# A two-layer attention encoder on one core: layer B's bias rows built by GpSimd, its bias loads in four transfers, and several steps of layer B moved

## The chip, the cores and the metric

The kernel runs on one core of a Trainium2 chip. The core has a matrix engine (PE), VectorE (DVE), ScalarE (ACT), GpSimd (POOL) and a queue engine (SP, SyncE), each with its own stream of instructions worked off in order, and 16 DMA engines. The metric is the device time of one execution in microseconds; lower is better.

## The reference

One sequence of 512 tokens of width 1024 goes through two layers. Each normalises its input, projects it to queries, keys, values and a gate, mixes by attention with 16 heads of 64, multiplies by silu(gate), projects back and adds the residual. Layer A attends in three dilated windows; layer B, the one that the change is mostly about, attends in a window of 8 by 16 on an 8 by 64 grid:

```python
def mixer_b(hn, w_in, w_out, q_gain, k_gain, rpb):
    proj = hn @ w_in
    q, k, v, gate = jnp.split(proj, 4, axis=-1)
    q = rms_norm(q..., q_gain) * (HEAD_DIM ** -0.5)
    k = rms_norm(k..., k_gain)
    ...
    bias = col_bias[:, row_idx].transpose(0, 2, 3, 1, 4)      # from rpb, by relative row and column
    logits = jnp.einsum('bhcqd,bhrcjd->bhcqrj', qr, kr).astype(jnp.float32) + bias
    logits = jnp.where(col_valid[:, :, None, :], logits, NEG_INF)
    p = softmax(logits)
    out = jnp.einsum('bhcqrj,bhrcjd->bhcqd', p, vr)
    ...
    y = y * jax.nn.silu(gate)
    return y @ w_out
```

All is float32.

## The kernel before

Every large product is made of three matmuls: each factor is split into a high part, rounded, and a low part, the rest (`wh`, `wl` of the raw weights `wraw`; `hn_h`, `hn_l` of the normalised input; the two halves of `y`), and the three products that matter are added in PSUM. ACT rounds the high parts of weights (L136), DVE or GpSimd subtracts for the low ones (L142). All matmuls go through one helper, L231.

The 16 heads form eight pairs, called hc 0 to 7. PE's order is written by hand with a clock of the plan: each matmul issued adds its estimated nanoseconds, and the attention of the pairs (the side work) is woven into the projections (the main work). `later_on(delay, job)` issues a job when that clock has advanced by `delay`; `B_PLAN` lists, for layer B, when the `scores` and the `values` of each pair come, in nanoseconds after layer B's start. The other engines' order comes from a scheduler, except where `tc.keep_in_program_order` pins an instruction. Nearly all DMAs are issued from SP's one queue, in order; each also waits for a DMA eight places before it to have landed.

In layer B a pair goes through these steps. Its Q and K are normalised (`head_norm`, on GpSimd or, with `quick`, with the root on DVE), written to DRAM (`bd<-rawq`, L738) and read back transposed (`rawq<-bd` or `vv<-bd` by the tile's name, L744; both in `move_b`). `side_b` scales the keys into `kx` on ACT (L776), copies two end blocks of `kx` (L1247), and after a time of the plan issues the scores (`log<-kx`, 64 small matmuls). DVE adds the bias `eb` and takes the maximum (L1275), ACT takes the exponential and divides (L1285, L1290). P is transposed (`turn_b`), written to `tdb` (L1225) and read back as `pt` (L1230). `values` then are `weigh` (`o<-pt`) and `put_y`: ACT and DVE copy and add the output (L791, L792), DVE multiplies by the gate (L846, tiles `gt` or `gx`), ACT rounds y's high part (L849), GpSimd or DVE subtracts for the low part (L852). y is a factor of the output projection at the end of the layer.

The bias `eb` (two buffers, by hc % 2) is read for one pair by eight DMAs of 80 KB (`eb<-eb_d`, L881, `bias_b`), issued at the start of the pair before. `eb_d`, in DRAM, is put together once during layer A by `bias_rows`: the table is loaded as `rp`, negated, widened by a fill value, written to two DRAM buffers, and 14 DMAs from DRAM to DRAM, one every 12000 ns of the plan, lay out its blocks.

The last residual (`pt<-xm_d`, L1173) is read in two halves into the halves of the `pt` buffer that P^T of pairs 6 and 7 leave. `tr` is the buffer, a single one, in which layer A's transposed P are gathered before they are written.

Of the kernel before, what the change touches and what calls it, by code (L numbers as in the profile page):

```python
# [22 lines left out]
P = 128  # L23
# [3 lines left out]
NHC = 8  # L27
# [19 lines left out]
    ("scores", 0, 47700), ("scores", 1, 70000), ("values", 0, 82000), ("scores", 2, 87000),  # L47
    ("values", 1, 108000), ("scores", 3, 108700), ("values", 2, 117000), ("scores", 4, 125400),
    ("scores", 5, 145000), ("values", 3, 145000), ("scores", 6, 165000), ("values", 4, 166000),
    ("scores", 7, 176700), ("values", 5, 180000), ("values", 6, 198000), ("values", 7, 207000),  # L50
# [5 lines left out]
def tile_hybrid_encoder(  # L56
# [39 lines left out]
    lb_d = dr.tile([P, 376], F32, name="lb_d")  # L96
    gb_d = dr.tile([P, 248], F32, name="gb_d")
    eb_d = dr.tile([P, 4, EB], F32, name="eb_d")
# [362 lines left out]
    def bias_rows():  # L461

        rp = wk.tile([P, 248], F32, tag="eg", name="rp")
        tc.keep_in_program_order(nc.sync.dma_start(rp, rpb))
        nc.gpsimd.tensor_scalar(rp, rp, -1.0, None, op0=ALU.mult)
        lb = wk.tile([P, 376], F32, tag="eg", name="lb")
        nc.gpsimd.memset(lb, BIG)
        nc.gpsimd.tensor_copy(lb[:, 15 * 8 : 31 * 8], rp[:, 7 * 8 : 23 * 8])
        nc.sync.dma_start(gb_d, rp)
        nc.sync.dma_start(lb_d, lb)  # L470

        far, near = (lb_d, 376), (gb_d, 248)
        jobs = [(2 * W5 + W5 * n, W5, far, 120) for n in range(4)]
        jobs += [(o, 32, far, 24) for o in (0, W5, 7 * W5 - 32, 8 * W5 - 32)]
        jobs += [(32, 32, near, 216), (64, 96, near, 120), (W5 + 32, P, near, 88)]
        jobs += [(6 * W5, P, near, 56), (7 * W5, 96, near, 56), (7 * W5 + 96, 32, near, 24)]

        def spread_out(o, n, src, at):
            t, width = src
            dst = bass.AP(eb_d.tensor, eb_d.offset + o, [[4 * EB, P], [EB, 4], [1, n]])  # L480
            src = bass.AP(t.tensor, t.offset + at, [[width, P], [-8, 4], [1, n]])
            tc.keep_in_program_order(nc.sync.dma_start(dst, src))

        for n, job in enumerate(jobs):
            later_on(30000 + 12000 * n, partial(spread_out, *job))
# [23 lines left out]
    def project_qk(n, ns, key, hc, guard, first=False, **kw):  # L509
# [219 lines left out]
    def move_b(hc):  # L729
# [17 lines left out]
        out, back = (6000, 13500) if hc % 2 else (14000, 20500)  # L747
# [73 lines left out]
    def put_y(hc, o, permuted, last):  # L821
# [33 lines left out]
        if permuted and hc < NHC - 3:  # L855
            later_on(9000, finish)
        else:
            finish()
# [14 lines left out]
    def bias_b(hc):  # L873

        def load(j, hd):
            src = bass.AP(
                eb_d.tensor,
                eb_d.offset + (2 * hc + hd) * 32 * EB + (0, 2, 2, 4)[j] * W5,
                [[EB, 4], [4 * EB, 8], [1, 4 * W5]],
            )  # L880
            tc.keep_in_program_order(nc.sync.dma_start(st["eb"][32 * j : 32 * j + 32, hc % 2, hd, :], src))  # L881

        for j in range(4):
            for hd in range(2):
                load(j, hd)
# [35 lines left out]
    def attn_a(hc):  # L921
# [115 lines left out]
        if hc < NHC - 1:  # L1037
            for u in range(2):
# [199 lines left out]
    def side_b(hc):  # L1238
        if hc >= 1 and hc + 1 < NHC:
            bias_b(hc + 1)  # L1240
# [6 lines left out]
        nc.gpsimd.tensor_copy(sb(kx, 0, [[576, 2], [1, 64]]), sb(kx, 128, [[320, 2], [1, 64]]))  # L1247
        yield 3500
# [67 lines left out]
        later_on(7500, partial(send_b, hc, pt))  # L1316
        pending.append(lambda: put_y(hc, weigh(), False, hc == NHC - 1))
# [25 lines left out]
    def side():  # L1343
# [22 lines left out]
        for hc in range(NHC):  # L1366
            if hc < NHC - 1:
# [147 lines left out]
```

## Time and profile before

| | |
|---|---|
| time, median of 3 runs | 810.78 us (814.51, 810.78, 810.58) |
| profiled execution, its own time | 816.14 us |
| its span | 814.3 us |
| mean granted clock of PE | 0.996 |
| PE busy | 799.7 us (98%) |
| DVE, ACT, POOL busy | 527.0, 441.3, 228.8 us |
| DMA | 172.14 MB, mean 211 GB/s |

The span is the profiled execution from its first to its last instruction; 1.84 us of its time lie around it. The profiled execution was 5.36 us longer than the median of the others. Busy time counts work of an engine; waits are listed apart, by what ended them.

### The profile page before, as it was taken

How to read it: one execution, taken by the hardware profiler on the slowest of the kernel's cores; microseconds unless marked ns; L12 is line 12 of the kernel's file. 1: busy time of each engine (PE TensorE's matmuls, PEld its weight loads, DVE VectorE, ACT ScalarE, POOL GpSimd, SP SyncE). 2: the span in 40 equal slices, each digit the busy share in tenths (PEclk: the TensorE clock that was granted, in tenths of full speed). 3: DMA queues.
4: the chain of work that ended last, by engine and by line, in shares of the span. 5: the costliest groups of instructions: out<-in, count | busy, mean ns of one | idle time of the engine just before them, and what ended most of it. 6: DMA issues, size and time to landing. Idle time of an engine off the chain costs nothing. (4 is left out here: it accounts for less than half of the span.)

```text
span 814.3 us, 17799 instructions
## 1 busy us (share of the span) xinstructions
PE 799.7 (98%) x6718; PEld 655.7 (81%) x6718; DVE 527.0 (65%) x1398; ACT 441.3 (54%) x925; POOL 228.8 (28%) x373
## 2 busy tenths in 40 slices
PE   9999999999999999999999999999999998999887
PEld 7888888888888888888888888888888786878776
DVE  7474575675675675676676776557648777786634
ACT  7442745645645745745746575454346666656520
POOL 2242432432442432432433232120403133220100
PEclk9999999999999999999999999999999999999999
DMA  8579578768987987877978963284556696777663
GB/s 288 159 205 259 149 220 257 232 195 234 247 225 215 293 243 217 260 221 220 283 212 238 282 179 113 61 280 155 176 158 168 209 220 199 237 214 216 199 171 145
DMA packets 96694, 172.14 MB, mean 211 GB/s; under 512 B 16288, under 2 KB 52272, under 8 KB 96608
## 3 DMA queue, kind: packets, MB, share of 16 engines
q1 hardware_dynamic: 96464, 170.74, 71.3%
q8 instruction: 53, 0.87, 0.5%
q10 hardware_dynamic: 144, 0.26, 0.1%
q14 instruction: 33, 0.27, 0.1%
HBM read 128.36 MB, written 48.24 MB: 217 GB/s over the span
## 5 line engine op out<-in xcount | busy, mean ns | idle before, releaser
L231 PE MATMUL acc<-wh,hn_h 128*128 128x512 f32 x704 | 278.2, 396 | 0.4 <-ACT hn_h L419 0.4
L231 PE MATMUL acc<-wl,hn_h 128*128 128x512 f32 x704 | 274.3, 390 | 0.2 <-POOL wl L142 0.2
L231 PE MATMUL acc<-wh,hn_l 128*128 128x512 f32 x704 | 274.2, 390 | 0.0
L136 ACT CAST wh<-wraw 128x512 fp32r<-128x512 f32 (+1 forms) x258 | 157.7, 614 | 211.7 <-PE acc L231 184.1
L142 DVE TENSOR_TENSOR wl<-wraw,wh 128x512 fp32r<-128x512 f32 (+2 forms) x187 | 136.9, 733 | 159.6 <-ACT wh L136 159.0
L142 POOL TENSOR_TENSOR wl<-wraw,wh 128x512 fp32r<-128x512 f32 (+1 forms) x72 | 96.5, 1340 | 227.0 <-ACT wh L136 177.6
L231 PEld LDWEIGHTS acc<-wh,hn_h 128*128 128x128 f32 x704 | 132.6, 189 | 32.6 <-issue 4.2
L231 PEld LDWEIGHTS acc<-wh,hn_l 128*128 128x128 f32 x704 | 132.4, 188 | 27.9
L231 PEld LDWEIGHTS acc<-wl,hn_h 128*128 128x128 f32 x704 | 132.7, 188 | 27.4 <-POOL wl L142 0.9
L309 POOL TENSOR_TENSOR sq<-rawq 128x256 f32<-128x256 f32 (+1 forms) x82 | 59.9, 739 | 110.4 <-ACT rawq L540 97.9
L231 PE MATMUL acc<-y,wh 128*128 128x512 f32 (+1 forms) x272 | 82.3, 386 | 2.0 <-ACT y L849 1.8
L992 ACT ACTIVATE p<-p,mn 128x512 f32<-128x512 f32 (+1 forms) x64 | 44.9, 702 | 60.2 <-DVE mn L981 60.2
L231 PE MATMUL acc<-hn_h,wh 128*128 128x512 f32 x192 | 75.8, 395 | 1.5 <-ACT rawk L540 1.5
L231 PE MATMUL acc<-hn_h,wl 128*128 128x512 f32 x192 | 74.8, 390 | 0.0
L231 PE MATMUL acc<-hn_l,wh 128*128 128x512 f32 x192 | 74.8, 389 | 0.0
L310 DVE TENSOR_REDUCE ss<-sq 128x4 f32<-128x256 f32 (+1 forms) x96 | 47.6, 506 | 32.2 <-POOL sq L309 31.7
L231 PEld LDWEIGHTS acc<-y,wh 128*128 128x128 f32 x272 | 49.0, 189 | 12.2 <-ACT y L849 2.2
L231 PE MATMUL acc<-y,wl 128*128 128x512 f32 (+1 forms) x136 | 51.4, 378 | 0.0
L329 DVE TENSOR_TENSOR rawq<-rawq,rs 128x256 f32<-128x256 f32 (+1 forms) x96 | 48.2, 563 | 2.3 <-POOL rs L128 1.9
L540 ACT ACTIVATE rawq<-acc,rs_n 128x512 f32<-128x512 f32 (+1 forms) x76 | 46.1, 613 | 0.5
L900 DVE STREAM_TRANSPOSE tr<-p 128x512 f32<-128x512 f32 x56 | 39.0, 706 | 11.4 <-ACT p L812 11.4
L812 ACT ACTIVATE p<-p,mn 128x512 f32<-128x512 f32 (+1 forms) x64 | 44.4, 701 | 2.1 <-DVE mn L811 2.1
(140 smaller groups left out, 911.4 us busy)
## 6 DMA issues: line engine op xcount, KB each, us to landing
wraw<-in_w SPq DMA_DIRECT2D x121, 512.0 KB
td<-tr SPq DMA_DIRECT2D x14, 1024.0 KB
pt<-td SPq DMA_DIRECT2D x56, 256.0 KB
qd<-rawq SPq DMA_DIRECT2D x7, 1536.0 KB
qt<-qd SPq DMA_DIRECT2D x28, 384.0 KB
tdb<-tb SPq DMA_DIRECT2D x8, 768.0 KB
pt<-tdb SPq DMA_DIRECT2D x32, 192.0 KB
eb<-eb_d SPq DMA_DIRECT2D x64, 80.0 KB
```

The source lines that it names most:

```text
L136: nc.scalar.copy(h, raw)
L142: eng.tensor_sub(l, raw, h.bitcast(F32))
L231: nc.tensor.matmul(o, l, r, **kw)
L309: nc.gpsimd.tensor_mul(to, v, v)
L310: nc.vector.tensor_reduce(ss[:, i * ns : (i + 1) * ns], sq.rearrange("p (a b) -> p a b", b=64), axis=AX.X, op=ALU.add)
L329: m = nc.vector.tensor_mul(v, v, by)
L540: nc.scalar.activation(dst, src, AF.Copy, scale=rs_n[:, i : i + 1])
L812: nc.scalar.activation(pr, pr, AF.Copy, scale=mn[:, 3:4])
L900: nc.vector.transpose(dst, src[:, :n].rearrange(order, b=4, k=32, **({"g": 2} if apart else {})))
L992: nc.scalar.activation(row, row, AF.Exp, bias=mn[:, 1:2], scale=-1.0, accum_out=mn[:, 2:3])
```

## The change

- `bias_rows(cq)` is called four times in layer A, once for each of four blocks of columns, behind the second half of the attention of hc 2 to 5. It loads the table into a tile in the `tr` buffer, and 4000 ns later GpSimd fills the 1280 columns of bias rows beside it: one memset, seven negating copies. 16000 ns after the start one DMA of 640 KB writes them to `eb_d`. The two DRAM buffers and the 14 DMAs are gone.
- `bias_b` reads a pair's bias in four DMAs of 160 KB, and is issued 4000 ns after the pair before last (the one that used the same buffer) is through its softmax.
- In `side_b` the end blocks of `kx` are copied by ACT, pinned in order, and 5000 ns of the plan lie between the keys and the scores, before 3500.
- For pairs 6 and 7 the second `head_norm` comes 11500 ns after its cause, before 18000, with its root on DVE. Pair 7's read back comes 12500 ns on, before 13500.
- `put_y` of layer B rounds y 4000 ns later, for pairs 0 to 5.
- The first half of the last residual is read behind pair 7's read of P^T, before: behind pair 6's values.
- `B_PLAN` has other times.

```diff
@@
 )
 B_OUT = B_IN + 4 * KT * D
 B_PLAN = (
-    ("scores", 5, 145000), ("values", 3, 145000), ("scores", 6, 165000), ("values", 4, 166000),
-    ("scores", 7, 176700), ("values", 5, 180000), ("values", 6, 198000), ("values", 7, 207000),
...
+    ("scores", 5, 143500), ("values", 3, 151500), ("scores", 6, 160500), ("values", 4, 168000),
+    ("scores", 7, 171500), ("values", 5, 182000), ("values", 6, 193000), ("values", 7, 199000),
 )
 W_COLS = B_OUT + KT * D
 
@@
     l0_d = dr.tile([16, P, 256], F32, name="l0_d")
     lines_d = dr.tile([16, 2, 448], F32, name="lines_d")
     l12_d = dr.tile([16, 2, 32, 224], F32, name="l12_d")
-    lb_d = dr.tile([P, 376], F32, name="lb_d")
-    gb_d = dr.tile([P, 248], F32, name="gb_d")
-    eb_d = dr.tile([P, 4, EB], F32, name="eb_d")
+    eb_d = dr.tile([16, 32, EB], F32, name="eb_d")
 
     v0x = cp.tile([P, 1024], F32, name="v0x")
     v0 = [v0x[:, 512 * i : 512 * i + 512].rearrange("p (i c) -> p i c", i=4) for i in range(2)]
@@
         for n, job in enumerate(jobs):
             later_on(3000 + 500 * n, partial(spread_out, *job))
 
-    def bias_rows():
-
-        rp = wk.tile([P, 248], F32, tag="eg", name="rp")
+    def bias_rows(cq):
+
+        t = wk.tile([P, 2048], F32, tag="tr", name="rows", bufs=1)
+        row, rp = t[:, :EB], t[:, EB : EB + 248]
         tc.keep_in_program_order(nc.sync.dma_start(rp, rpb))
-        nc.gpsimd.tensor_scalar(rp, rp, -1.0, None, op0=ALU.mult)
-        lb = wk.tile([P, 376], F32, tag="eg", name="lb")
-        nc.gpsimd.memset(lb, BIG)
-        nc.gpsimd.tensor_copy(lb[:, 15 * 8 : 31 * 8], rp[:, 7 * 8 : 23 * 8])
-        nc.sync.dma_start(gb_d, rp)
-        nc.sync.dma_start(lb_d, lb)
-
-        far, near = (lb_d, 376), (gb_d, 248)
-        jobs = [(2 * W5 + W5 * n, W5, far, 120) for n in range(4)]
-        jobs += [(o, 32, far, 24) for o in (0, W5, 7 * W5 - 32, 8 * W5 - 32)]
-        jobs += [(32, 32, near, 216), (64, 96, near, 120), (W5 + 32, P, near, 88)]
-        jobs += [(6 * W5, P, near, 56), (7 * W5, 96, near, 56), (7 * W5 + 96, 32, near, 24)]
-
-        def spread_out(o, n, src, at):
-            t, width = src
-            dst = bass.AP(eb_d.tensor, eb_d.offset + o, [[4 * EB, P], [EB, 4], [1, n]])
-            src = bass.AP(t.tensor, t.offset + at, [[width, P], [-8, 4], [1, n]])
-            tc.keep_in_program_order(nc.sync.dma_start(dst, src))
-
-        for n, job in enumerate(jobs):
-            later_on(30000 + 12000 * n, partial(spread_out, *job))
+
+        def fill():
+            nc.gpsimd.memset(row, BIG)
+            jobs = [(2 * W5 + 8 * cq, [[W5, 4], [1, P]], 56, [[0, 4], [1, P]])]
+            for o, n, at in (
+                (32, 32, 216), (64, 96, 120), (W5 + 32, P, 88),
+                (6 * W5, P, 56), (7 * W5, 96, 56), (7 * W5 + 96, 32, 24),
+            ):
+                jobs.append((o, [[1, n]], at - 8 * cq, [[1, n]]))
+            for o, to, at, of in jobs:
+                nc.gpsimd.tensor_scalar(sb(row, o, to), sb(rp, at, of), -1.0, None, op0=ALU.mult)
+
+        def write():
+            dst = eb_d.rearrange("h (c r) x -> c h r x", c=4)[cq]
+            tc.keep_in_program_order(nc.sync.dma_start(dst, row))
+
+        later_on(4000, fill)
+        later_on(16000, write)
 
     st = {}
     pq = wk.tile([P, 4096], F32, tag="pt", name="pt", bufs=1)
@@
                 squares(blocks_of(i, "raw1"), ss2, i, 4)
             move = [partial(move_b, 2 * hc + f) for f in range(2)]
             head_norm("raw0", ss, 4, 0, True, then=move[0])
-            head_norm("raw1", ss2, 4, 18000, then=move[1])
+            head_norm("raw1", ss2, 4, 18000 if hc < 3 else 11500, hc == 3, then=move[1])
             for n in range(2):
                 stamp[key, 2 * hc + n] = clock[0]
             return
@@
             tc.keep_in_program_order(nc.sync.dma_start(dst, src))
             left[0] -= 1
 
-        out, back = (6000, 13500) if hc % 2 else (14000, 20500)
+        out, back = (6000, 12500) if hc == NHC - 1 else (6000, 13500) if hc % 2 else (14000, 20500)
         later_on(out, write)
         for a in (0, 2, 1, 3):
             later_on(back, partial(read, a))
@@
 
         if permuted and hc < NHC - 3:
             later_on(9000, finish)
+        elif not permuted and hc < NHC - 2:
+            later_on(4000, finish)
         else:
             finish()
 
@@
 
     def bias_b(hc):
 
-        def load(j, hd):
-            src = bass.AP(
-                eb_d.tensor,
-                eb_d.offset + (2 * hc + hd) * 32 * EB + (0, 2, 2, 4)[j] * W5,
-                [[EB, 4], [4 * EB, 8], [1, 4 * W5]],
-            )
-            tc.keep_in_program_order(nc.sync.dma_start(st["eb"][32 * j : 32 * j + 32, hc % 2, hd, :], src))
-
+        src = eb_d[2 * hc : 2 * hc + 2].rearrange("h p x -> p h x")
         for j in range(4):
-            for hd in range(2):
-                load(j, hd)
+            o = (0, 2, 2, 4)[j] * W5
+            m = nc.sync.dma_start(st["eb"][32 * j : 32 * j + 32, hc % 2], src[:, :, o : o + 4 * W5])
+            tc.keep_in_program_order(m)
 
     class turner:
 
@@
                     turned.put(pr, 512, 256 * hd + 64 * (t % 2), 128)
                 send = partial(turned.send, pq[:, 2048 * u : 2048 * u + 2048], *((6000, 500) if u else (8500, 1200)))
                 later_on(7000 + 2000 * u, send)
+                if u and 2 <= hc < 6:
+                    later_on(12000, partial(bias_rows, hc - 2))
                 if pending and u == 0:
                     yield 7500
                     pending.pop(0)()
@@
             later_on(7500 + 500 * i, partial(read, n))
 
     def side_b(hc):
-        if hc >= 1 and hc + 1 < NHC:
-            bias_b(hc + 1)
         landed, left = st.pop(("raw", hc))
         assert not left[0]
         e = st["eb"][:, hc % 2]
         kx = wk.tile([P, 20 * 32], F32, tag="e12", name="kx")
         mid = kx[:, 64 : 64 + S].rearrange("p (i t r) -> p t i r", i=4, t=4)
         tc.keep_in_program_order(scaled(mid, landed[:, :, 1, :].rearrange("p t (i r) -> p t i r", i=4), 3))
-        nc.gpsimd.tensor_copy(sb(kx, 0, [[576, 2], [1, 64]]), sb(kx, 128, [[320, 2], [1, 64]]))
-        yield 3500
+        ends = nc.scalar.copy(sb(kx, 0, [[576, 2], [1, 64]]), sb(kx, 128, [[320, 2], [1, 64]]))
+        tc.keep_in_program_order(ends)
+        yield 5000
         pt = pq[:, 2048 * (hc % 2) : 2048 * (hc % 2) + 4 * RUN]
 
         def scores(u):
@@
         for args in held:
             turn_b(*args)
         later_on(7500, partial(send_b, hc, pt))
+        if hc + 2 < NHC:
+            later_on(4000, partial(bias_b, hc + 2))
         pending.append(lambda: put_y(hc, weigh(), False, hc == NHC - 1))
 
     def main():
@@
                 half = attn_a(hc)
                 for v in half:
                     if v == "half":
-                        if hc == 2:
-                            bias_rows()
                         halves.append(half)
                         break
                     yield v
@@
             if job == "scores":
                 yield from side_b(hc)
                 continue
+            if hc == NHC - 1:
+                yield "wait", ("back", hc), 0
+                yield from residual(xm_d, 0)
             yield "wait", ("back", hc), 3500
             if hc == NHC - 2:
                 stamp["yb", "turned"] = 0
             pending.pop(0)()
             yield
-            if hc >= NHC - 2:
-                yield from residual(xm_d, 4 * (hc % 2))
+            if hc == NHC - 1:
+                yield from residual(xm_d, 4)
 
     run(main(), side())
```

Counted in matmuls of 512 columns on PE, the scores of pairs 2, 3, 4, 6 and 7 stand at 2517, 2607, 2676, 2832 and 2877 (before 2520, 2616, 2679, 2847, 2892), those of pair 5 at 2763 (before 2766); the values of pairs 1 and 7 at 2574 and 2982 (before 2595 and 3000). The first matmul with y of pair 7 is number 3006 in both, the last of all 3072.

How instructions move, at three places. ACT, around the scores of pair 3: the rows from the casts of weights (`wh`) ahead of the copy of pair 1's output (`ow`) to those behind the keys (`kx<-vv`). Before:

```order
L136 CAST wh<-wraw 128x512 x3
L1207 ACTIVATE eg<-gx 128x512
L791 COPY ow<-o 128x512
L136 CAST wh<-wraw 128x512
L849 CAST y<-gt 128x512
L776 ACTIVATE kx<-vv,gk 128x4x4x32
L136 CAST wh<-wraw 128x512
L1285 ACTIVATE p,mns<-p,mns 128x160 x4
```

and after:

```order
L536 ACTIVATE rawq<-acc,rs_n 128x16x32 x4
L134 CAST wh<-wraw 128x512
L787 COPY ow<-o 128x512
L134 CAST wh<-wraw 128x512
L772 ACTIVATE kx<-vv,gk 128x4x4x32
L845 CAST y<-gt 128x512
L1239 COPY kx<-kx 128x2x64
L134 CAST wh<-wraw 128x512
L1201 ACTIVATE eg<-gx 128x512
L134 CAST wh<-wraw 128x512
```

The scaling of the keys now comes ahead of y's rounding, and the copy of the ends is on ACT, behind it.

SP, around the reads of K and Q of pairs 6 (`rawq<-bd`) and 7 (`vv<-bd`). Before:

```order
L738 DMA bd<-rawq 128x4x256
L195 DMA wraw<-in_w 128x1024
L744 DMA rawq<-bd 32x4x256 x4
L1225 DMA tdb<-tb 128x4x384
L738 DMA bd<-rawq 128x4x256
L195 DMA wraw<-in_w 128x1024
L881 DMA eb<-eb_d 32x1x640 x8
L195 DMA wraw<-in_w 128x1024
L1230 DMA pt<-tdb 32x4x384
L744 DMA vv<-bd 32x4x256 x4
```

and after:

```order
L734 DMA bd<-rawq 128x4x256 x2
L876 DMA eb<-eb_d 32x2x640 x4
L193 DMA wraw<-in_w 128x1024
L740 DMA rawq<-bd 32x4x256 x4
L1219 DMA tdb<-tb 128x4x384
L740 DMA vv<-bd 32x4x256 x4
L193 DMA wraw<-in_w 128x1024
L1224 DMA pt<-tdb 32x4x384 x2
```

The write of pair 7 and the bias load now stand ahead of pair 6's read; pair 7's read has only a write of P between it and pair 6's.

SP, at the end, around the reads of P^T of pair 7 (`pt<-tdb`) and of the last residual (`pt<-xm_d`). Before:

```order
L1225 DMA tdb<-tb 128x4x384
L195 DMA wraw<-in_w 128x256
L195 DMA wraw<-in_w 128x512
L1173 DMA pt<-xm_d 128x1024 x2
L195 DMA wraw<-in_w 128x256
L1230 DMA pt<-tdb 32x4x384 x3
L195 DMA wraw<-in_w 128x1024
L1230 DMA pt<-tdb 32x4x384
L195 DMA wraw<-in_w 128x1024
L1173 DMA pt<-xm_d 128x1024 x2
```

and after:

```order
L1219 DMA tdb<-tb 128x4x384
L193 DMA wraw<-in_w 128x256
L193 DMA wraw<-in_w 128x512
L1224 DMA pt<-tdb 32x4x384 x4
L1167 DMA pt<-xm_d 128x1024 x2
L193 DMA wraw<-in_w 128x256
L193 DMA wraw<-in_w 128x1024
L1167 DMA pt<-xm_d 128x1024 x2
```

The residual's first half has moved behind all four reads of P^T.

More of the change, by code (lines that the diff above doesn't have):

```diff
@@ L46 @@
 B_PLAN = (
-    ("scores", 0, 47700), ("scores", 1, 70000), ("values", 0, 82000), ("scores", 2, 87000),
-    ("values", 1, 108000), ("scores", 3, 108700), ("values", 2, 117000), ("scores", 4, 125400),
-    ("scores", 5, 145000), ("values", 3, 145000), ("scores", 6, 165000), ("values", 4, 166000),
-    ("scores", 7, 176700), ("values", 5, 180000), ("values", 6, 198000), ("values", 7, 207000),
+    ("scores", 0, 46200), ("scores", 1, 68500), ("values", 0, 82000), ("scores", 2, 85500),
+    ("values", 1, 103500), ("scores", 3, 106500), ("values", 2, 119000), ("scores", 4, 123900),
+    ("scores", 5, 143500), ("values", 3, 151500), ("scores", 6, 160500), ("values", 4, 168000),
+    ("scores", 7, 171500), ("values", 5, 182000), ("values", 6, 193000), ("values", 7, 199000),
 )
```

## The prediction

> **What bounds the kernel now.** I read the page first. TensorE is busy almost throughout, so only its idle time and its clock can give anything:
>
> ```profile
> PE 799.7 (98%) x6718; PEld 655.7 (81%) x6718; DVE 527.0 (65%) x1398; ACT 441.3 (54%) x925; POOL 228.8 (28%) x373
> ```
>
> Then the table of PE's waits (total us, times, longest), which says what ended the idle time, and PE's timeline at those places (start, busy us, then in brackets the idle time ahead):
>
> ```profile
> PE log L231 <- POOL kx L1247: 5.0, 2, 2.6
> PE acc L231 <- ACT y L849: 1.8, 1, 1.8
> PE o L231 <- DMA pt<-tdb: 1.5, 1, 1.5
> PE acc L231 <- ACT rawk L540: 1.5, 1, 1.5
> ```
>
> ```profile
> 677.71 1.58 PE L231 MATMUL log<-kx,vv 64*32 64x160 f32 x64 [2.40 <-POOL kx L1247]
> ...
> 682.56 0.40 PE L231 MATMUL acc<-wh,hn_l 128*128 128x512 f32 x1
> 682.79 0.39 PE L231 MATMUL acc<-wh,hn_h 128*128 128x512 f32 x1
> ...
> 732.43 0.50 PE L231 MATMUL acc<-hn_h,wh 128*128 128x512 f32 x1 [1.46 <-ACT rawk L540]
> ...
> 741.51 1.34 PE L231 MATMUL log<-kx,rawq 64*32 64x160 f32 x64
> ...
> 743.35 0.40 PE L231 MATMUL acc<-hn_h,wl 128*128 128x512 f32 x1
> ...
> 757.56 2.49 PE L231 MATMUL log<-kx,vv 64*32 64x160 f32 x64 [2.58 <-POOL kx L1247]
> ...
> 760.90 0.40 PE L231 MATMUL acc<-y,wl 128*128 128x512 f32 x1
> ...
> 790.01 1.65 PE L231 MATMUL o<-pt,rawk 64*64 64x128 f32 x64 [1.51 <-DMA pt<-tdb]
> 791.59 0.72 PE L231 MATMUL acc<-y,wh 128*128 128x512 f32 x2
> ...
> 795.05 0.49 PE L231 MATMUL acc<-y,wh 128*128 128x512 f32 x1 [1.81 <-ACT y L849]
> 795.78 0.50 PE L231 MATMUL acc<-y,wh 128*128 128x512 f32 x1 [0.23 <-DVE y L852]
> ```
>
> So there are five places, all in layer B (ahead of it only the start has any over 0.5): scores of pair 3 (2.40), a gate block (1.46), scores of pair 7 (2.58), the output of pair 7 (1.51) and the first use of its y (1.81 and 0.23): 9.99 us. Two of them cost more than the wait. The third view is the windows of PE (stretch, its us, busy, granted clock, DMA share, GB/s):
>
> ```profile
> 680.00:684.00 4.00, 4.00 (x15) 0.72 0.71 226
> 756.00:760.00 4.00, 2.44 (x65) 0.67 0.89 270
> 792.00:796.00 4.00, 1.96 (x8) 1.00 0.74 246
> ```
>
> The clock falls behind the waits of 2.40 and 2.58 and stays at 1.00 behind the one of 1.81. Undisturbed, a score block and two matmuls behind it take 743.35 - 741.51 = 1.84 us, and a matmul 0.23 (682.56 to 682.79). For pair 7 the same stretch took 760.90 - 757.56 = 3.34: 1.5 too much. For pair 3 a block and eight matmuls took 682.56 - 677.71 = 4.85 instead of 1.84 + 6 x 0.23 = 3.2: 1.65 too much. So the five places cost 9.99 + 3.15 = 13.1 us. The profiled execution took 816.14 us, so a kernel without any of them stands at 803.0 on that footing.
>
> **The change, place by place.** Scores of pair 3. Who made the key late stands in the rows of ACT and POOL:
>
> ```profile
> 670.42 0.59 ACT L791 COPY ow<-o 128x512 f32<-128x512 f32 x1 [0.18 <-PE o L231]
> ...
> 675.00 0.62 ACT L849 CAST y<-gt 128x512 fp32r<-128x512 f32 x1 [1.92 <-DVE gt L846]
> 675.52 0.72 ACT L776 ACTIVATE kx<-vv,gk 128x512 f32<-128x512 f32 x1
> 675.69 1.27 POOL L852 TENSOR_TENSOR y<-gt,y 128x512 fp32r<-128x512 f32 x1
> 676.90 0.76 POOL L1247 COPY kx<-kx 128x128 f32<-128x128 f32 x1
> 679.02 0.43 ACT L1285 ACTIVATE p<-p,mns 128x160 f32<-128x160 f32 x1 [2.28 <-DVE mns L1275]
> ```
>
> The scaling of the keys stood behind y's rounding, which waited 1.92 us for VectorE, and the copy of the key's ends stood behind y's low part on GpSimd. Now the scaling goes ahead of y, and the ends are copied by ACT. That copy has 128 columns; its nearest row on ACT is 0.43 for 160 columns, against 0.76 on GpSimd. The scores stand at large matmul 2607, behind pair 1's output at 2574, so 33 x 0.23 = 7.6 us are left for the copy of the output, the scaling, y and the ends. Here alone y still stands between scaling and ends, so the ends still wait for gt; y went out 4.6 us behind its output's copy before (670.42 to 675.00), and 0.62 + 0.43 makes some 5.7 of the 7.6. I take the wait and its slow clock as gone: -4.05.
>
> The gate block. The bank it needs is emptied by ACT (the L540 of the table of waits) behind y, and y waits for VectorE, which comes to gx late:
>
> ```profile
> 730.49 0.65 DVE L846 TENSOR_TENSOR gx<-gx,ow 128x512 f32<-128x512 f32 x1
> ```
>
> The pair's output is computed sooner against this place and y's rounding is issued 4 us of the plan later. Between -1.46 and nothing; -1.3, since a move of a few us outweighs 1.46.
>
> Scores of pair 7. The chain of waits (first two lines) and SP's timeline:
>
> ```profile
> 740.59 9.48 DMA eb<-eb_d
> 750.08 6.25 DMA vv<-bd
> ```
>
> ```profile
> 731.71 1.74 SPq L744 DMA_DIRECT2D rawq<-bd  x4
> 735.74 8.17 SPq L881 DMA_DIRECT2D eb<-eb_d  x8
> 777.42 0.80 SPq L1173 DMA_DIRECT2D pt<-xm_d  x2
> ```
>
> Eight bias transfers hold SP for 8.17 us, each waiting for one eight back to land; behind them stands the read of pair 7's K and Q (vv), whose landing takes 6.25. After it, that read no longer has the bias load directly in front and its write is some 7.5 us sooner in the plan (18 to 11.5 and 13.5 to 12.5). The scores stand 15 matmuls sooner (2877, before 2892), 3.4 us, and lose the 1.46 above as room: they ask for 2.58 + 3.4 + 1.46 = 7.4 us, and get from 7.5 to 7.5 + 8.17 = 15.7. Gone: -4.1.
>
> Output of pair 7. Its four reads of P^T (which follow 777.42) stood behind the first half of the last residual, whose buffer comes free only with the output of pair 6; the chain gives their landing as
>
> ```profile
> 780.78 9.09 DMA pt<-tdb
> ```
>
> Now they are ahead of it. The output stands 18 matmuls sooner (2982, before 3000), 4.1 us, with the scores 3.4 sooner, so the room shrinks by 0.7 only. Gone: -1.5. What is late next is the residual, whose halves go out behind these reads and behind the output block, 90 x 0.23 = 20.7 us ahead of the last matmul, against a landing of 9.1: covered.
>
> First use of y of pair 7: still at matmul 3006, now 24 x 0.23 = 5.5 us behind the output instead of six matmuls. From 791.59 to 795.78, 4.2 us, is what the chain needs: -2.04.
>
> **What is new.** (a) GpSimd fills the bias rows four times in layer A. The nearest rows, and a weight's low part with the matmul that reads it:
>
> ```profile
> 218.48 0.41 POOL L467 MEMSET lb<- 128x376 f32 x1
> 228.32 0.83 POOL L465 TENSOR_SCALAR rp<-rp 128x248 f32<-128x248 f32 x1 [9.43 <-DMA rp<-in_rpb]
> 261.95 1.29 POOL L142 TENSOR_TENSOR wl<-wraw,wh 128x512 fp32r<-128x512 f32 x1 [4.01 <-ACT wh L136]
> ```
>
> ```profile
> 268.70 0.39 PE L231 MATMUL acc<-wl,hn_h 128*128 128x512 f32 x1
> ```
>
> The fill of 1280 columns scales to 1.4, the seven negations with 1024 columns to 3.4: 4.8 us, up to 6 if each has a start of its own. GpSimd was idle for 4.01 there and its product is used 268.70 - 263.24 = 5.5 us later: nothing on PE, which has no wait in this stretch. If the fill waits for its row of rpb too (9.43 above), GpSimd stands still; the cover then is gone, and PE waits some 4 us each time. The buffer is that of the transposed blocks, so VectorE may wait 1 to 2 us for the write; that lies under PE as well. The 16 small transfers that put the rows together before are gone from SP, and cost nothing there.
>
> (b) The bias load is now issued right behind a pair's softmax, in four transfers; it stands ahead of the read of the next K and Q on SP, where it stood behind. The nearest rows for pairs 6 and 4 are the keys' scaling and, for pair 4, the scores:
>
> ```profile
> 735.84 0.72 ACT L776 ACTIVATE kx<-rawq,gk 128x512 f32<-128x512 f32 x1
> ...
> 691.36 0.72 ACT L776 ACTIVATE kx<-rawq,gk 128x512 f32<-128x512 f32 x1
> ```
>
> ```profile
> 696.85 1.34 PE L231 MATMUL log<-kx,rawq 64*32 64x160 f32 x64
> ```
>
> Pair 6: the key is ready at 735.84 + 0.72 + 0.4 = 737.0, its scores at 741.51: 4.5 us of room. The scores move 15 matmuls up (3.4) and the wait of 1.46 goes: 4.9. That is a wait of 0.4 if the read leaves as before, and 4.5 if half of the 8.17 comes in front of it (four transfers for eight). SP waited anyway ahead of 731.71, and the load comes early in that gap, so I take 0.8. Pair 4: 696.85 - 692.5 = 4.4 of room, nine matmuls up (2.1), and the 4.05 of pair 3 gone: 1.75 short if nothing else moves, nothing if the read follows PE and moves up too. Its time hangs on PE's progress through the plan in part: 0.7. Together 1.5, between 0 and 6.
>
> Sum: 816.14 - 4.05 - 1.3 - 4.1 - 1.5 - 2.04 + 1.5 = 804.6. The median shown is 5.36 under the profiled execution; the three runs differ among themselves by 3.9, the size of one of the two dear waits, so most of the 5.36 is likely waits that go anyway. The slowest, 814.51, is 1.6 under the profiled one, which I take as the profile's own. 804.6 - 1.6 = 803.0. If all 5.36 were the profile's own, it would be 799.2.
>
> **The clock's price by the notes.** Its rows are the windows above. The Trainium skill, "TensorE: Matmul & The Clock Gate", section "Part 1: The HAM clock gate (the "warmup" mystery)", says that a free-running monitor with a window of about 3.4 us halves the clock after at least one idle window. Read strictly, gaps of 2.40 and 2.58 would not do it, and the trace disagrees, unless the thin stretch of score matmuls counts as idle. By that rule the sum loses the 3.15 for the clock.
>
> **Rivals.** First, the two small new waits are large: the reads of pairs 4 and 6 land late enough that each wait passes 2.4 and closes the clock, 2.4 + 1.55 each, 7.9 instead of 1.5: 809.4. For it: the room is used up on paper. Against: SP has slack ahead of both reads. 0.15. Second, the slow matmuls have a cause of their own (DMA share 0.89 stands beside clock 0.67) and stay, the waits go: 803.0 + 3.15 = 806.2. Against: the share 0.74 stands beside 1.00. 0.08. Third, the change does not do what it says at its two dear places: the ends of pair 3 still wait behind y, and pair 7's read is late again because its scores moved up by as much: 803.0 + 8.1 = 811.1. 0.07. Fourth, slower: the bias load's packets, not its issue, delay the read behind it. If the read of K and Q lands behind the load, 9.48 instead of 6.25 and an issue of 4.1 ahead, pairs 4 and 6 are 7.3 later each; SP's gap takes up some, I count 6.5 and 1.5 for the clock, 8 us twice, against 1.5 in the sum: 803.0 + 14.5 = 817.5. It decides from 13.3 us of new waits on (11.8 more than in the sum). For it, the chain already shows a read behind a load; against, that load was eight transfers. 0.10.
>
> **How the numbers follow.** A measurement of this kernel tells about 0.5% from no change: faster is under 806.7, slower over 814.8. The forecast (all five places go, new waits of 0 to 3 us) has 0.60 and 803.0, by itself 799 to 806. Faster 0.60 + 0.08 = 0.68, same 0.15 + 0.07 = 0.22, slower 0.10. The range goes from 799.0 (all 5.36 kept) to 810.5, which takes in the first two rivals and leaves out the last two and a little below.
>
> **What would show it.** Right: no wait of PE over 1 us at the scores of pairs 3 and 7, the output of pair 7 and its y; the granted clock at 1.00 throughout layer B; PE's busy time about 3 us less; small waits at scores 4 and 6 for ACT's kx; layer A without waits. Wrong: waits on wl from GpSimd in layer A, waits over 2 us at scores 2, 4 or 6 for the read of K and Q, or slow matmuls without a wait ahead of them.

## The result: slower by 1.2%, and the profile after

The changed kernel takes 821.35 us (820.72 to 822.89), the kernel before, on the same chip, 811.8 (810.58 to 814.51). The ratio is 1.0116, 95% interval 1.0084 to 1.0147. The forecast was 803.0, with a range to 810.5: wrong. The profiled execution took 821.26 us, its span is 819.5.

The page's line of busy times, and the table of PE's waits:

```profile
PE 803.0 (98%) x6718; PEld 656.5 (80%) x6718; DVE 528.4 (64%) x1409; ACT 442.1 (54%) x933; POOL 239.5 (29%) x380
```

```profile
PE acc L229 <- POOL wl L140: 6.4, 3, 2.4
PE tp L233 <- DVE rawq L327: 2.6, 1, 2.6
PE log L229 <- ACT kx L1239: 1.9, 1, 1.9
PE busy L393 <- DVE warm L382: 0.9, 1, 0.9
PE acc L229 <- DVE wl L140: 0.6, 1, 0.6
PE acc L229 <- ACT rawk L536: 0.5, 1, 0.5
PE log L229 <- DVE ow L788: 0.2, 1, 0.2
```

None of the five places of before is left. There is a new one at scores 6 (kx), as forecast, and new ones that were not: weights' low parts from GpSimd and a late rawq. PE's timeline says where they are (first line of layer B: `pk<-ones,ssq`, the sums of squares ahead of it):

```profile
270.95 0.50 PE L229 MATMUL acc<-wl,hn_h 128*128 128x512 f32 x1 [2.44 <-POOL wl L140]
...
334.27 0.50 PE L229 MATMUL acc<-wl,hn_h 128*128 128x512 f32 x1 [1.53 <-POOL wl L140]
...
398.45 0.50 PE L229 MATMUL acc<-wl,hn_h 128*128 128x512 f32 x1 [2.39 <-POOL wl L140]
...
501.60 1.39 PE L233 MATMUL tp<-ident,rawq 128*128 128x128 f32 x4 [2.57 <-DVE rawq L327]
...
578.83 0.95 PE L229 MATMUL pk<-ones,ssq 128*128 128x1 f32 x8
...
749.89 2.19 PE L229 MATMUL log<-kx,rawq 64*32 64x160 f32 x64 [1.86 <-ACT kx L1239]
```

and the same line of before:

```profile
563.39 0.95 PE L231 MATMUL pk<-ones,ssq 128*128 128x1 f32 x8
```

All but the last lie in layer A. Layer B begins 15.44 us later (578.83 against 563.39), and the kernel's span ends 5.2 later (819.5 against 814.3): layer B became 10.2 us shorter, and layer A, which had no wait of PE behind its start, 15.4 longer. At each of the four places in layer A stands one of the four fills of the bias rows. GpSimd's rows at the first, and SP's:

```profile
256.15 1.29 POOL L140 TENSOR_TENSOR wl<-wraw,wh 128x512 fp32r<-128x512 f32 x1 [1.97 <-issue]
268.51 1.16 POOL L466 MEMSET rows<- 128x1280 f32 x1 [11.06 <-DVE wl L140]
269.63 1.26 POOL L140 TENSOR_TENSOR wl<-wraw,wh 128x512 fp32r<-128x512 f32 x1
271.08 3.81 POOL L474 TENSOR_SCALAR rows<-rows 128x512 f32<-128x512 f32 x7 [0.19 <-DMA rows<-in_rpb]
```

```profile
258.06 0.38 SPq L901 DMA_DIRECT2D td<-tr  x1
...
268.42 0.33 SPq L463 DMA_DIRECT2D rows<-in_rpb  x1
```

The memset's tile `rows` lies in the buffer of `tr`, and the transfer `td<-tr`, issued at 258.06, was still reading that buffer. The memset was at the head of GpSimd's queue from 257.4 and held it for 11.06 us, with a low part of a weight behind it. The profile names DVE's wl as what ended the wait. That the read ended it is inferred here: SP's load into the same buffer, which waits for the same read, left at 268.42. At the second fill the profile names the read itself:

```profile
331.81 1.17 POOL L466 MEMSET rows<- 128x1280 f32 x1 [10.14 <-DMA td<-tr]
```

At the first fill wl came at 269.63 instead of some 261.9, and PE, which has 5.5 us of room there, waited 2.44.

At the fourth place the fill (459.56, behind 5.61 of waiting) held the squares of another projection's heads, and the delay ran through DVE to the transposes at 501.60:

```profile
459.56 1.17 POOL L466 MEMSET rows<- 128x1280 f32 x1 [5.61 <-DMA td<-tr]
```

```profile
461.76 0.69 DVE L308 TENSOR_REDUCE ss<-sq 128x8 f32<-128x512 f32 x1 [7.09 <-POOL sq L307]
```

### The profile page after: what moved, and what is told of

Its sections match the earlier page's. It is cut to its first block, busy times and chain, and to the rows that moved or that the text cites. A ratio compares the mean times of both kernels' runs of the same rounds, so it can differ in the third digit from the quotient of the medians.

```text
span 819.5 us, 17778 instructions
## 1 busy us (share of the span) xinstructions
PE 803.0 (98%) x6718; PEld 656.5 (80%) x6718; DVE 528.4 (64%) x1409; ACT 442.1 (54%) x933; POOL 239.5 (29%) x380
## 4 chain that ended last, share of the span: by engine, by line
PE 45%; DMA 10%; DVE 7%; issue 2%; ACT 1%; POOL 1%; SPq 0%; POOLq 0%; ACTq 0%
PE acc L229 39%; PE o L229 3%; DMA wraw<-in_w 2%; PE log L229 2%; DMA td<-tr 2%; DVE wl L140 2%; DMA qd<-rawq 2%; DVE rawq L327 1%; DMA qt<-qd 1%; DMA bd<-rawq 1%; PE tp L233 1%; DMA rawq<-bd 1%; DMA eb<-eb_d 1%; DVE na L121 1%; POOL wl L140 1%
```

## The experiments

Theory 1: the fill waits for the shared buffer, and GpSimd's queue, worked off in order, holds the weights' low parts behind it. Theory 2: the fill's own 5 us of work, four times, are what makes them late. Theory 3: the transfers (the loads of the table and the writes to `eb_d`) cost the time.

**Other buffers.** The fill lies in buffers that are free in layer A, one pair earlier:

```diff
-        t = wk.tile([P, 2048], F32, tag="tr", name="rows", bufs=1)
-        row, rp = t[:, :EB], t[:, EB : EB + 248]
+        CUT = 6 * W5
+        low = slot(KT - 2, "rows", F32)[:, :CUT]
+        t = slot(KT - 3, "rows2", F32)
+        top, rp = t[:, : EB - CUT], t[:, EB - CUT : EB - CUT + 248]
...
-            nc.gpsimd.memset(row, BIG)
+            tc.keep_in_program_order(nc.gpsimd.memset(low, BIG))
+            tc.keep_in_program_order(nc.gpsimd.memset(top, BIG))
...
-                if u and 2 <= hc < 6:
-                    later_on(12000, partial(bias_rows, hc - 2))
+                if u and 1 <= hc < 5:
+                    later_on(12000, partial(bias_rows, hc - 1))
```

> The changed kernel, but the bias rows are put together in buffers that nobody else uses then (the y buffers of pairs 6 and 5, 960 and 320 columns, two writes to eb_d in place of one), one pair earlier in layer A; GpSimd does the same fill of some 5 us, four times. Theory 1, the fill waits for the shared buffer (the read of tr by td<-tr) and GpSimd's queue holds the weights' low parts behind it: the waits on wl in layer A and the ones near 480 to 502 us vanish, with their slow clock 15.4 us, so 821.4 - 15.4 = 806, and no wait of PE over 0.6 us in layer A. Theory 2, the 5 us of work on GpSimd are what makes wl late: three waits on wl of over 1 us stay, 816 to 822. Theory 3, the transfers (table load and 640 KB writes on SP) are what costs: they are all still there, 818 to 822.

It took 815.45 us, ratio 1.0042 (1.0026 to 1.0058). The waits on wl and near 480 to 502 are gone, as theory 1 has it; another came, of the experiment's own making, since pair 5 needs one of these buffers for its queries while the fourth write still reads it (ACT's row there waited 9.96 us for `eb_d<-rows`, a shared buffer again):

```profile
PE log L229 <- ACT q L777: 8.9, 1, 8.9
PE log L229 <- ACT kx L1244: 1.8, 1, 1.8
```

GpSimd at the place of the first fill of the changed kernel:

```profile
261.35 1.29 POOL L140 TENSOR_TENSOR wl<-wraw,wh 128x512 fp32r<-128x512 f32 x1 [4.14 <-ACT wh L134]
264.55 1.34 POOL L307 TENSOR_TENSOR sq<-rawq 128x256 f32<-128x256 f32 x2 [1.91 <-ACT rawq L541]
265.83 0.90 POOL L468 MEMSET rows<- 128x960 f32 x1
```

There is no wait ahead of the fill, and the work is the same. The fill also stands behind wl here, since its memset was pinned in program order. So two things changed at once; a later run takes that up.

**Layer A's part alone, layer B's part alone.** First the kernel before with the new rows, its eight bias transfers reading the new layout:

```diff
-        rp = wk.tile([P, 248], F32, tag="eg", name="rp")
...
+        t = wk.tile([P, 2048], F32, tag="tr", name="rows", bufs=1)
...
-                [[EB, 4], [4 * EB, 8], [1, 4 * W5]],
+                [[EB, 32], [1, 4 * W5]],
```

> The kernel before with the new bias rows alone (GpSimd's fill in the shared buffer, four writes to eb_d; layer B and its eight bias transfers as before). If layer A's part costs what the traces put there (15.4 us at the start of layer B) and layer B does not care: 811 + 15 = 826, with PE's waits on wl at the same three places. If the loss comes from layer B's new order: 810 to 813.

It took 826.9 us, ratio 1.0171 (1.015 to 1.0193): the loss is that part's, as expected. Layer B began at 578.19, 14.8 later than before. From there to the end of the span it took 246.5 us against 250.9 before, though its order was not touched; the last experiment comes back to that.

Then the changed kernel with the old rows, whose layout in DRAM makes eight transfers a pair necessary:

```diff
-        t = wk.tile([P, 2048], F32, tag="tr", name="rows", bufs=1)
...
+        rp = wk.tile([P, 248], F32, tag="eg", name="rp")
...
-        src = eb_d[2 * hc : 2 * hc + 2].rearrange("h p x -> p h x")
+        def load(j, hd):
```

> The changed kernel with the old bias rows (one table load, 14 DRAM-to-DRAM transfers) and so eight bias transfers a pair, in the new place; all else of layer B as changed. Theory 1 and 2: layer A has no wait, layer B keeps the 10.2 us that it gains between the traces, so 821.4 - 15.4 = 806 (between 802 and 808, since eight transfers may be later than four for scores 6). If the two parts of the change need each other: over 812.

It took 813.5 us, ratio 0.9997 (0.9979 to 1.0014): a miss. Layer A was as before and layer B began at 562.97, but layer B gained little. From its start to the end of the span it took 248.9 us, against 250.9 before and 240.7 in the changed kernel. Its waits:

```profile
PE log L231 <- DMA vv<-bd: 6.5, 1, 6.5
PE acc L231 <- ACT rawq L540: 2.6, 1, 2.6
```

The wait of 6.5 us is that of scores 6. The profile names pair 7's read for it, but the keys were late on ACT, for pair 6's read, which left behind a bias load of eight issues on SP:

```profile
740.52 0.72 ACT L776 ACTIVATE kx<-rawq,gk 128x512 f32<-128x512 f32 x1 [8.95 <-DMA rawq<-bd]
```

```profile
724.51 6.67 SPq L883 DMA_DIRECT2D eb<-eb_d  x8
732.06 2.04 SPq L744 DMA_DIRECT2D rawq<-bd  x4
```

**Twice the fill**, in buffers of its own:

```diff
-        def fill():
+        def fill(again=True):
+            if again:
+                fill(False)
```

> As the kernel with buffers of its own, but each fill is done twice (10 us of GpSimd in place of 5). Theory 1: the room for wl is 4.0 idle and 5.5 slack at the first place, so a fill of 10 us just passes it: 0 to 2 us a fill, 0 to 8 us above the single fill. Theory 2: the second fill costs as much as the first, four times 3 to 4 us: 14 us above.

816.58 us, ratio 1.006 (1.0041 to 1.0079), 1.1 above the single fill, with no wait on wl over 0.4 us. The wait of pair 5's queries grew from 8.9 to 11.4, which is more than the whole difference. Apart from that wait, twice the work on GpSimd cost PE nothing: theory 2 falls.

**The fills one pair sooner still**, which takes the experiment's own wait away:

```diff
-                if u and 1 <= hc < 5:
-                    later_on(12000, partial(bias_rows, hc - 1))
+                if u and hc < 4:
+                    later_on(12000, partial(bias_rows, hc))
```

> As the kernel with buffers of its own for the bias rows, but the four fills stand one pair sooner (hc 0 to 3, there hc 1 to 4), so that the last is over before pair 5 of layer A needs one of these buffers for its queries (the wait of 8.93 us before log<-qt,q there). Theory 1 (only the shared buffer cost the time): 815.4 less 8.9 and about 1.5 of slow clock, so 805, with no wait over 0.6 us in layer A and 1.8 at scores 6. If the fill or its transfers cost something of their own: 808 or more, with waits on wl.

804.83 us, ratio 0.9891 (0.9851 to 0.993): as theory 1 has it. The transfers are all there, so theory 3 falls too. Its waits, and the start of its layer B, which comes 0.6 us sooner than before and 16 sooner than in the changed kernel:

```profile
PE log L229 <- ACT kx L1244: 1.6, 1, 1.6
PE busy L393 <- DVE warm L382: 0.9, 1, 0.9
```

```profile
562.78 0.95 PE L229 MATMUL pk<-ones,ssq 128*128 128x1 f32 x8
```

**The shared buffer, but a later fill**, behind the low parts in GpSimd's queue:

```diff
-            nc.gpsimd.memset(row, BIG)
+            nc.gpsimd.tensor_scalar(row, sb(rp, 0, [[0, 8], [1, W5]]), 0.0, BIG, op0=ALU.mult, op1=ALU.add)
...
-        later_on(16000, write)
+        later_on(9000, write)
...
-                    later_on(12000, partial(bias_rows, hc - 2))
+                    later_on(19000, partial(bias_rows, hc - 2))
```

> The changed kernel with the shared buffer kept; the load of the table and the fill come 7 us later in the plan (the write to eb_d as before), and the fill value is written by a tensor_scalar that reads the loaded table in place of the memset, so that on GpSimd it can't be put ahead of the weights' low parts any more. The fill gets longer, some 8 us for 5. Theory 1 (the stall on the buffer ahead of wl): the three waits on wl vanish though GpSimd works more, 806 to 811. Theory 2 (the work itself): the waits grow, 822 to 832.

831.38 us, ratio 1.021 (1.0161 to 1.0258): 10 above the changed kernel, where I expected 10 to 15 below. The time lies in the range that was put down for theory 2. The trace does not bear that out: the fill took 1.26 + 4.80 us, one more than in the changed kernel, not three. GpSimd again stood for 10.46 us, now in the midst of the squares and for the table:

```profile
264.57 0.63 POOL L307 TENSOR_TENSOR sq<-rawq 128x256 f32<-128x256 f32 x1 [1.91 <-ACT rawq L536]
275.65 1.26 POOL L466 TENSOR_SCALAR rows<-rows 128x1280 f32<-128x1280 f32 x1 [10.46 <-DMA rows<-in_rpb]
```

```profile
267.83 1.75 SPq L905 DMA_DIRECT2D pt<-td  x4
269.63 0.53 SPq L463 DMA_DIRECT2D rows<-in_rpb  x1
```

The table's load needs the shared buffer too and was issued behind the reads of P^T, which wait for `td<-tr`. wl itself was now on time (GpSimd at 261.37), and what stood behind the fill, squares and the next wl, was late; its waits on wl summed to 9.4 from GpSimd and 8.3 from DVE. So what matters is that GpSimd's queue stands, whatever it is that stands behind: theory 1 in a wider form. In the kernels with own buffers nothing held the fill, and nothing was lost ahead of layer B once the fills stood early enough. A kernel with own buffers and the memset ahead of wl was not run.

**Layer B, part by part**, each against the kernel with own buffers and sooner fills (804.83).

The residual's first half back ahead of pair 7's P^T:

```diff
-            if hc == NHC - 1:
-                yield "wait", ("back", hc), 0
-                yield from residual(xm_d, 0)
...
-            if hc == NHC - 1:
-                yield from residual(xm_d, 4)
+            if hc >= NHC - 2:
+                yield from residual(xm_d, 4 * (hc % 2))
```

> As the kernel with buffers of its own and sooner fills, but the first half of the last residual is read where it was before, ahead of pair 7's reads of P^T on SP. If that place made the output of pair 7 wait, as the prediction has it: a wait of about 1.5 us for pt<-tdb at the output of pair 7, 1.5 above. If the later scores alone had made it late: no wait, the same time.

805.11 us, ratio 0.9906 (0.9874 to 0.9939). The time can't tell it, the trace does, with the wait back:

```profile
PE log L229 <- ACT kx L1244: 2.1, 1, 2.1
PE o L229 <- DMA pt<-tdb: 1.0, 1, 1.0
```

The keys' ends on GpSimd again:

```diff
-        ends = nc.scalar.copy(sb(kx, 0, [[576, 2], [1, 64]]), sb(kx, 128, [[320, 2], [1, 64]]))
-        tc.keep_in_program_order(ends)
+        nc.gpsimd.tensor_copy(sb(kx, 0, [[576, 2], [1, 64]]), sb(kx, 128, [[320, 2], [1, 64]]))
```

> As the kernel with buffers of its own and sooner fills, but the end blocks of the keys are copied by GpSimd, not pinned, as before. If GpSimd's copy behind y's low part was what made the scores of pair 3 late: a wait for kx of 0.5 to 2.5 us there, up to 4 above with the slow clock. If the scaling's place on ACT was the larger part: no wait there, the same time, and the wait at scores 6 grows by 0.3, the longer copy.

803.5 us, ratio 0.9875 (0.9837 to 0.9912), no wait at scores 3, and 1.5 at scores 6 as before. That the ends moved to ACT was not needed, with all else as changed.

y rounded at once:

```diff
-        elif not permuted and hc < NHC - 2:
-            later_on(4000, finish)
```

> As the kernel with buffers of its own and sooner fills (804.8), but y is rounded at once in layer B, not 4 us later. If that delay is what took the wait of 1.46 at the gate block away: a wait of 0.5 to 1.5 for rawk or for kx on ACT comes back, 1 to 2 above; with one ahead of the keys of pair 3 up to 4. If the other moves had done it: no wait, the same time.

805.3 us, ratio 0.9914 (0.9892 to 0.9936), the gate block does not wait, and there is one more wait of 0.2 for kx. The delay was not needed either, with all else as changed.

The normalisation of pairs 6 and 7, and pair 7's read, at their old times:

```diff
-            head_norm("raw1", ss2, 4, 18000 if hc < 3 else 11500, hc == 3, then=move[1])
+            head_norm("raw1", ss2, 4, 18000, then=move[1])
...
-        out, back = (6000, 12500) if hc == NHC - 1 else (6000, 13500) if hc % 2 else (14000, 20500)
+        out, back = (6000, 13500) if hc % 2 else (14000, 20500)
```

> As the kernel with buffers of its own and sooner fills (804.8), but the second head_norm of pairs 6 and 7 comes 18000 ns after its cause with the root on GpSimd, and pair 7's read back 13500 ns on, as before. The prediction wanted 7.4 us of room at scores 7, of which 7.5 came from this move: without it a wait of 2 to 7 us at scores 7 for vv<-bd, with the slow clock 3 to 8 above. If the bias load's new place alone had made the room (8.2 us): no wait at scores 7, same time; the write of pair 7 then leaves SP's way ahead of scores 6, and the wait there goes.

801.61 us, ratio 0.987 (0.9848 to 0.9892). Scores 7 don't wait, and scores 6 don't either:

```profile
PE busy L393 <- DVE warm L382: 0.9, 1, 0.9
PE acc L229 <- POOL wl L140: 0.4, 1, 0.4
```

Its SP, and that of the changed kernel, around the bias load of pair 7:

```profile
714.98 0.38 SPq L739 DMA_DIRECT2D bd<-rawq  x1
...
716.90 2.29 SPq L881 DMA_DIRECT2D eb<-eb_d  x4
722.13 1.73 SPq L745 DMA_DIRECT2D rawq<-bd  x4
```

```profile
730.66 6.71 SPq L734 DMA_DIRECT2D bd<-rawq  x2
737.43 2.45 SPq L876 DMA_DIRECT2D eb<-eb_d  x4
741.11 1.89 SPq L740 DMA_DIRECT2D rawq<-bd  x4
```

With the sooner normalisation, pair 7's write stands directly behind pair 6's on SP and waits for its data; that holds the bias load and pair 6's read, which follow it in the queue. The row of two writes takes 6.71 us from the first to the end of the second.

The other way to the same end, with the ends on GpSimd, moves pair 7's bias load behind both reads:

```diff
-            later_on(4000, partial(bias_b, hc + 2))
+            later_on(10000 if hc == 5 else 4000, partial(bias_b, hc + 2))
```

> As the kernel with buffers of its own, sooner fills and the keys' ends on GpSimd (803.5), but pair 7's bias load is issued 6 us later in the plan, so that it stands on SP behind the reads of K and Q of pairs 6 and 7, no longer ahead of them. If the load in front is what makes scores 6 late (1.5 to 2.1 us there in three kernels): that wait goes, since four issues of 3.0 us leave the way, 801.9, and the bias still lands some 6 us before the scores of pair 7 are done. If the read itself, or the write of pair 7 that stands ahead, is the cause: 803.5 and the wait stays.

801.82 us, ratio 0.9874 (0.9856 to 0.9892), no wait over 0.4 behind the start's 0.9: as expected. With pair 7's write still ahead the wait is gone too, so taking either the write or the load away is enough. These two are the fastest versions here, 10 us below the kernel before.

Eight bias transfers a pair, rows from GpSimd:

```diff
-            o = (0, 2, 2, 4)[j] * W5
-            m = nc.sync.dma_start(st["eb"][32 * j : 32 * j + 32, hc % 2], src[:, :, o : o + 4 * W5])
+            for hd in range(2):
+                o = (0, 2, 2, 4)[j] * W5
+                m = nc.sync.dma_start(
+                    st["eb"][32 * j : 32 * j + 32, hc % 2, hd, :], eb_d[2 * hc + hd][:, o : o + 4 * W5]
+                )
```

> As the kernel with buffers of its own and sooner fills (804.8), but a pair's bias is read in eight transfers of 80 KB again, in the same new place; so it differs from the kernel with layer B alone (813.5) only in who put the rows together. If the number of transfers is what made scores 6 wait 6.5 us there and a matmul 2.6 us at scores 4's place: both come back, 812 to 814. If it was the rows' older place in DRAM, or the 14 transfers of layer A: 804 to 806, and scores 6 waits under 2.5.

807.0 us, ratio 0.9919 (0.9894 to 0.9945), and 2.5 us at scores 6: near the second reading. Eight transfers in place of four cost 2 us by the medians and 1.1 by the spans (802.8 against 801.7), and the intervals of the ratios overlap; so the cost is small if there is one. The other 6.5 of the 8.7 between layer B's part alone (813.5) and 804.83 go with the old rows, whose issues took 609 ns at the median against 416 here.

The kernel with layer A's part alone narrows that down. Its layer B has the order and the eight transfers of the kernel before, and reads only the new layout of `eb_d`: each transfer takes 32 rows in one step, `[EB, 32]`, where the old one took them as `[EB, 4], [4 * EB, 8]`. An issue takes 420 ns at the median against 609 before, the eight of pair 7 hold SP for 5.22 us against 8.17, and the wait of 2.58 at scores 7 is gone. SP's row of that load, and the windows of PE over the later half of it, before and then with the new layout:

```profile
746.18 5.22 SPq L877 DMA_DIRECT2D eb<-eb_d  x8
```

```profile
740.00:744.00 4.00, 4.00 (x76) 3.02 (x76) 2.05 (x11) 1.88 (x8) 0.00 (x0) 1.00 0.28 106
748.00:752.00 4.00, 4.00 (x20) 3.26 (x19) 1.39 (x2) 2.48 (x5) 0.29 (x1) 1.00 0.95 255
```

With the old layout the DMA engines are busy for 0.28 of the time there, with the new one for 0.95, in part with a read of weights issued at 745.63. So a good part of the cost goes with the way in which the rows are read. The 14 transfers of layer A can hardly be the cause, since the last is issued at 430.9. Why the old pattern leaves the engines idle stays open.

## Why the prediction was wrong

**The step that failed is (a) of what is new**, GpSimd's fill, with nothing on PE. Its size was right: 4.8 to 6 us forecast, 5.0 measured (1.16 + 3.81). The cover was right as well, as the double fill shows. What was wrong is that GpSimd would start the fill as soon as it came to it. The text asked whether the fill might wait for the table's row, and priced that at some 4 us of PE each time; it said of the shared buffer only that DVE may wait for the write. That the fill itself must wait until the buffer's earlier content is read was missed. The consequence is the one that the text describes for the table: GpSimd stands still, and wl behind it is late. PE lost 2.7, 1.8, 4.3 and 7.0 us at the four fills. These are the steps by which the same blocks of PE fall behind in this trace; it was 0.4 ahead until then, which makes 15.4 in all. Four times the text's 4 us is close to that, but it had named another cause for it, and gave it no place in the sum and no chance. The nearest rival, the slower one, named the bias load in layer B. Its signs of being wrong did name waits on wl from GpSimd in layer A, and those came. The rows that would have told it were there. In the kernel before, the transfer that reads `tr` at this place is followed 12 us later by the reads of its result, which wait for it:

```profile
257.17 0.38 SPq L909 DMA_DIRECT2D td<-tr  x1
...
269.38 1.75 SPq L913 DMA_DIRECT2D pt<-td  x4
```

**The rest of the sum** held in total, not term by term. Its -13.0 and +1.5 make -11.5 for layer B, between traces; measured were -10.2 in the changed kernel and -12.0 in the kernel with the fill out of the way (238.9 us against 250.9). That the latter's median, 804.83, lies beside the sum's 804.6 is in part luck. The sum starts from one profiled execution, at 816.14, and by medians that kernel gained 8.2 us (813.02 to 804.83). The 3.15 us of slow clock belong to that execution as well: of 41 others of the kernel before, in the experiments, five show a granted clock of 1.000, and took 810.42 to 811.51. The allowance of 1.6 for the profile itself was not borne out: 816.14 lies within those 41 (810.42 to 817.29), and the changed kernel's profiled execution within its own runs.

Scores 3, the gate block, scores 7, output 7, its y: all five waits are gone, as forecast. The reasons were only partly right. Scores 3: not for the ends' move to ACT; what is left is the keys' place ahead of y and the sooner output of pair 1, and neither was tried alone. The gate block: not for y's later rounding; what did it is open. Scores 7: the 7.5 us of sooner normalisation that the sum counted on were not needed; with the bias load out of the way the read was early enough, and with layer A's part alone the new layout took the wait away even with the load in front. Output 7: the place of the reads did it, as forecast, worth 1.0 where 1.5 was taken.

Scores 6: a wait came where it was forecast, of 1.86 us against 0.8, with the slow clock behind it in the changed kernel; the cause is the write of pair 7 and the bias load together, where the text named the load alone. Scores 4: no wait, where 0.7 was forecast.

Of the rivals, the first (two large new waits in layer B) and the third did not happen. The fourth's mechanism, a read behind the bias load, appeared with eight transfers in layer B's part alone, at 6.5 us.

## What the runs showed of the clock

The granted clock in windows of the changed kernel, behind waits of 2.44 and 2.39, and of layer A's part alone behind one of 1.85 (stretch, us, busy of PE, PEld, DVE, ACT, POOL, then clock, DMA share, GB/s):

```profile
269.00:273.00 4.00, 2.05 (x9) 1.72 (x10) 0.17 (x1) 1.67 (x3) 3.81 (x5) 1.00 0.88 224
397.00:403.00 6.00, 4.55 (x13) 3.60 (x14) 0.22 (x1) 1.31 (x3) 6.00 (x11) 0.72 0.97 246
```

```profile
336.00:340.00 4.00, 3.59 (x10) 2.87 (x11) 0.00 (x0) 0.72 (x2) 4.00 (x8) 0.65 1.00 267
```

I had read from the profile before that a gap from some 2.4 us on drops the clock. It does not go by length: 2.44 left it at 1.00, 2.39 and 1.85 did not. Each drop costs about 1.5 us, by the prediction's two places. The Trainium skill, "TensorE: Matmul & The Clock Gate", section "Part 1: The HAM clock gate (the "warmup" mystery)", calls the monitor's window free-running; that the same gap acts now one way, now the other agrees with it. That one whole idle window of about 3.4 us is needed does not agree with these rows.

The traces show more, which was not tested. In windows of 1 us each drop of the changed kernel reads 0.50 for some 3.4 us, and the three begin at about 398.8, 501.2 and 750.4: 102.4 and 249.2 us apart, 30 and 73 times 3.413. So the clock seems to be set on a fixed grid of 3.41 us. The gap of 2.44 lies across a line of that grid (at 269.1: 0.6 us ahead of it, 1.8 behind), and the gap of 2.39 within one step. Where a gap falls in the grid would then count beside its length.

## What to carry to other kernels

An instruction put on an engine with slack brings its wait along: before the busy time is counted as covered, find what last uses the buffer that it writes, when that use ends in the trace, and what stands behind the instruction in the engine's queue. Here 5 us of work a fill were free, and standing for 5.6 to 11.1 us at each of four fills cost 15.4 us. A profile shows such a wait as idle time of an engine with much idle time; the sign is the bracket on the fill's row, not the busy share, and the engine named in the bracket can be the wrong one.
